# Reading turned tiles back by quarters of the row: one core, two layers of a decoder trunk

## The chip, the core and the metric

The kernel runs on 1 core of one Trainium2 chip. The metric is the device time of one execution in microseconds (us). The profile's engine names are used: PE is TensorE (matmuls; PEld its weight loads), DVE is VectorE, ACT is ScalarE, POOL is GpSimd and SP is SyncE. POOL, SP and ACT also issue transfers (DMAs).

## The reference, cut

Two layers of a decoder trunk with 256 tokens of width 1024, in float32. Each layer: half a SwiGLU block, a token mixer, attention over 256 memory tokens, half a SwiGLU block. Layer 0's mixer joins a gated short convolution with sliding-window attention of 8 heads; layer 1's is causal attention of 8 heads.

```python
def swiglu(x, w_gate, w_up, w_down):
    return (jax.nn.silu(x @ w_gate) * (x @ w_up)) @ w_down
...
for l in range(DEPTH):
    x = x + 0.5 * swiglu(rmsnorm(x, ffn1_norm[l]), ffn1_w_gate[l], ffn1_w_up[l], ffn1_w_down[l])
    h = rmsnorm(x, mix_norm[l])
    if l % 2 == 0:
        i = l // 2
        x = x + even_mixer(h, ev_w_in[i], ev_conv_w[i], ev_sinks[i], ev_w_out[i], rel_bias)
    else:
        i = l // 2
        x = x + odd_mixer(h, od_w_in[i], od_w_out[i], rel_bias)
    x = x + memory_cross_attention(rmsnorm(x, xa_norm[l]), mem_n, xa_w_q[l], xa_w_kv[l], xa_w_o[l])
    x = x + 0.5 * swiglu(rmsnorm(x, ffn2_norm[l]), ffn2_w_gate[l], ffn2_w_up[l], ffn2_w_down[l])
return rmsnorm(x, final_norm)
```

## The kernel before

**Precision by pairs.** Every float32 operand of a matmul is split into two fp32r tiles, hi (a rounded copy, by ACT) and lo (what is left, by DVE), and a product is made of three matmuls: hi by hi, hi by lo, lo by hi. Weights stream from DRAM in 1 MB chunks (`raw`, issued by SP at L117) and are split block by block, 8 tiles of 128x128 at a time, by ACT at L143 (`whi`) and DVE at L144 (`wlo`). Five buffers of each are kept, so ACT and DVE can work up to four blocks ahead of PE, and a split of a block waits until PE has used the block five places before it.

**Feed-forward blocks (`ffn`, four times).** The hidden layer is made with tokens on the partitions, 512 hidden columns at a time (L575 to L577). `turned_back` (L540) then brings it to hidden columns on the partitions, as the down-projection needs. DVE transposes 32x32 blocks inside a tile of 128x1024 (L545); the blocks have still to change places across groups of 32 partitions, so POOL writes the tile to a DRAM buffer `turn` (L547) and reads it back in four transfers that exchange the two block indices (L549). `split` (L553) runs later: ACT (L557) and DVE (L558) make hi and lo tiles `h` of the tile. There are 24 such turns in a run; the last one of each block is 128x512. The last feed-forward block keeps tokens on the partitions for its down-projection too (L792 to L794) and starts it right behind the hidden layer.

**Layer 0's attention (`even_mixer`).** Four head pairs are handled in turn. `attend_two` makes the scores (L1090 to L1092) and the softmax, then `weigh_two` turns the weights in the same way: blocks on DVE (L1033), write of the 128x768 tile `pT` to `pturn` by POOL (L1035), four reads (L1037), then `go_split` on ACT (L1051) and DVE (L1053) into tiles `p`, then `go_weigh`, six matmuls on PE (L1022 to L1024), and the store of the result as an `h` tile (L504, L506). Between these steps PE runs the projections (`group`, L423 to L425: three matmuls of 256 columns for one weight tile), the convolution's and the memory keys' among them. `out_proj` at the end multiplies the eight `h` tiles (four of the convolution, four of the attention) into eight column tiles of the output: first column tiles 0 to 3, then 4 to 7. Four PSUM tiles `acc` are shared by these; `add_to_x` (L486) empties one into the residual `x`.

**What sets the order.** `Order` is a planner: it holds a clock in nanoseconds, a list of filler pieces for PE with estimated costs, and tasks with due times (`pe.after(delay, task, cost)`). When a task is due it goes first, otherwise the next filler. The number 15500 at L1095 is the delay from issuing the reads to `go_split`. The tile framework's scheduler then lays out each engine's instructions, and every engine runs its own in order. POOL's order holds the writes and reads of all turns, with the big accumulated weight transfers of `load_bases` and `add` between them in three of the feed-forward blocks. The splits of a turn are pinned in program order (`tc.keep_in_program_order`). In `out_proj`, `early` cuts the eight inputs: with `()` each column tile takes all eight at once; with `(7,)` column tiles 0 to 3 take the first seven inputs, and then the eighth.

Of the kernel before, what the change touches and what calls it, by code (L numbers as in the profile page):

```python
# [240 lines left out]
def paired(t):  # L241

    return t.rearrange("p (b a) -> p a b", b=2)


def halves(t):

    return t.rearrange("p (b a) -> p b a", b=2)
# [17 lines left out]
def build(nc, tc, ctx, a):  # L266
# [12 lines left out]
    def tr_tile():  # L279
        return psum.tile([P, 512], F32, name="tr", bufs=2)  # L280
# [7 lines left out]
    def p2():  # L288
        return act.tile([P, 512], F32R, name="p2", bufs=4)


    x = consts.tile([P, KT, S], F32, name="x")
# [22 lines left out]
    pe = Order()  # L315
# [173 lines left out]
    def split_into(x2, src):  # L489

        nc.scalar.activation(x2.hi, src, AF.Copy)
        nc.vector.tensor_tensor(x2.lo, src, x2.hi.bitcast(F32), op=ALU.subtract)
        return x2

    def h_tile():
        return Split(act.tile([P, 2 * S], F32R, name="h", bufs=FT))
# [37 lines left out]
    def ffn(which, layer, n, nxt, first=False, last=False):  # L534
# [5 lines left out]
        def turned_back(f0, s, c):  # L540

            t = act.tile([P, 8 * c * 32], F32, name=(("v", "kT", "v", "k2", "kT", "v") if sevens else ("v", "k2") * 3)[f0 // 4], bufs=1)
            to = t.rearrange("p (b u c i) -> p u c b i", b=4, u=2, c=c)
            for u in range(2):
                nc.vector.transpose(to[:, u], s[u].rearrange("p (c b j) -> p c b j", c=c, b=4))  # L545
            d = dram.tile([P, 8 * c * 32], F32, name="turn", bufs=2)
            nc.gpsimd.dma_start(d, t)  # L547
            for b in range(4):
                nc.gpsimd.dma_start(t[32 * b:32 * b + 32].rearrange("j (a x) -> j a x", a=4),  # L549
                                   d.rearrange("(a j) (b x) -> b j a x", a=4, b=4)[b])  # L550
            back = t.rearrange("p (a u c i) -> p c u a i", a=4, u=2, c=c)

            def split():  # L553
                for i in range(c):
                    h[f0 + i] = x2 = h_tile()
                    hi, lo = (m.rearrange("p u (a i) -> p u a i", a=4) for m in (x2.hi, x2.lo))
                    tc.keep_in_program_order(nc.scalar.activation(hi, back[:, i], AF.Copy))  # L557
                    tc.keep_in_program_order(nc.vector.tensor_tensor(lo, back[:, i], hi.bitcast(F32), op=ALU.subtract))  # L558

            pe.after({0: 34000, 4: 34000, 8: 28000, SEVEN: 30000}.get(f0, 26000) if sevens else  # L560
                     28000 if f0 < FT // 4 * 4 - 4 else 22000, split, 0)
# [428 lines left out]
    def weigh_two(prs, v2, store, delay, by_dma):  # L990


        state = {}

        def go_turn():

            if turned:
                pe.after(400, go_turn, 0)
                return
            turned.append(True)  # L1000
            first, last = tr_tile(), tr_tile()
            for s, pr in enumerate(prs):
                for to, at in ((0, 0), (1, 1)):
                    nc.tensor.transpose(first[:, s * S + to * P:s * S + (to + 1) * P], pr[:, at * P:(at + 1) * P], ident)
            for s, pr in enumerate(prs):
                nc.tensor.transpose(last[:, s * P:(s + 1) * P], pr[:, 2 * P:3 * P], ident)
            hi, lo, end = p2(), p2(), p2()
            nc.scalar.activation(hi, first, AF.Copy)
            nc.vector.tensor_tensor(lo, first, hi.bitcast(F32), op=ALU.subtract)
            end = Split(end)  # L1010
            nc.scalar.activation(end.hi, halves(last[:, :S]), AF.Copy)
            nc.vector.tensor_tensor(end.lo, halves(last[:, :S]), end.hi.bitcast(F32), op=ALU.subtract)
            state["pT"] = (paired(hi), paired(lo)), (end.high, end.low)
            pe.after(1600, go_weigh, 1000)

        def go_weigh():
            turned.clear()
            out = tr_tile()
            for t, (ph, pl) in enumerate(state["pT"]):
                ps = out if t == 0 else out[:, S:]  # L1020
                vh, vl = v2(t)
                nc.tensor.matmul(ps, vh, ph, start=t == 0, stop=False)  # L1022
                nc.tensor.matmul(ps, vh, pl, start=False, stop=False)
                nc.tensor.matmul(ps, vl, ph, start=False, stop=t == 1)  # L1024
            store(out.rearrange("p (q s) -> p s q", s=2))
            ws.flush()

        def go_blocks():
            state["t"] = t = act.tile([P, 6 * P], F32, name="pT", bufs=3)
            to = t.rearrange("p (b n i) -> p n b i", b=4, n=6)  # L1030
            for s, pr in enumerate(prs):
                for out, at in ((to[:, 2 * s:2 * s + 2], slice(0, 2 * P)), (to[:, 4 + s:5 + s], slice(2 * P, 3 * P))):
                    tc.keep_in_program_order(nc.vector.transpose(out, pr[:, at].rearrange("p (n b j) -> p n b j", b=4, j=32)))  # L1033
            d = dram.tile([P, 6 * P], F32, name="pturn", bufs=2)
            nc.gpsimd.dma_start(d, t)  # L1035
            for b in range(4):
                nc.gpsimd.dma_start(t[32 * b:32 * b + 32].rearrange("j (a x) -> j a x", a=4),  # L1037
                                   d.rearrange("(a j) (b x) -> b j a x", a=4, b=4)[b])
            pe.after(by_dma, go_split, 0)

        def go_split():
            if turned:
                pe.after(400, go_split, 0)
                return
            turned.append(True)
            back = state["t"].rearrange("p (a n i) -> p n a i", a=4, n=6)
            hi, lo, end = p2(), p2(), Split(p2())
            pairs = [(hi.rearrange("p (n a i) -> p n a i", n=4, a=4), lo.rearrange("p (n a i) -> p n a i", n=4, a=4), back[:, :4]),
                     (*(m.rearrange("p s (a i) -> p s a i", a=4) for m in (end.hi, end.lo)), back[:, 4:])]
            for h, _, src in pairs:  # L1050
                tc.keep_in_program_order(nc.scalar.activation(h, src, AF.Copy))  # L1051
            for h, l, src in pairs:
                tc.keep_in_program_order(nc.vector.tensor_tensor(l, src, h.bitcast(F32), op=ALU.subtract))  # L1053
            state["pT"] = (paired(hi), paired(lo)), (end.high, end.low)
            pe.after(2000, go_weigh, 1000)

        if by_dma:
            pe.after(delay + 200, go_blocks, 0)
        else:
            pe.after(delay, go_turn, 700)  # L1060
# [15 lines left out]
    def attend_two(q, k2, v2, biases, sinks, done):  # L1076

        state = {}

        def go_scores():
            q2 = split_into(q2_tile(), halves(q))
            both = [sc_tile(), sc_tile()]
            for t in range(2):
                ps = both[t][:, :(t + 1) * S]
                kh, kl = (paired(k)[:, :(t + 1) * P] for k in k2)
                qh, ql = (q2.v[:, t, m] for m in range(2))
                nc.tensor.matmul(ps, qh, kh, start=True, stop=False)  # L1090
                nc.tensor.matmul(ps, qh, kl, start=False, stop=False)
                nc.tensor.matmul(ps, ql, kh, start=False, stop=True)  # L1092
            state["p"] = [softmax([ps[:, :(t + 1) * S].rearrange("p (k s) -> p s k", s=2)[:, s] for t, ps in enumerate(both)],
                                  biases[s], sinks[s]) for s in range(2)]
            weigh_two(state["p"], v2, store, 5600, 15500)  # L1095

        def store(out):
            x2 = h_tile()
            parts = [(slice(64 * s, 64 * s + 64), out[64 * s:64 * s + 64, s]) for s in range(2)]
            split_all([(x2.hi[r], x2.lo[r], halves(src)) for r, src in parts])  # L1100
            done(x2)

        pe.after(1400, go_scores, 1000)
# [126 lines left out]
    def even_mixer(n, nxt, bias, sinks, kv2, extra):  # L1230
        k2, v2 = kv2
        o = [None] * 8
# [69 lines left out]
        f = group(W, 0, 2048, n, evac_k) + group(W, 0, 2176, n, evac_v)  # L1302
# [6 lines left out]
            f += t  # L1309
        when_scaled(n, square_scale)  # L1310
        norm_scale(n)
        pe.run(f + extra + out_proj("ev_w_out", 0, o, nxt, ()))

    def odd_mixer(n, nxt, bias, extra):
        k2 = [h_tile() for _ in range(4)]
# [68 lines left out]
    nxt = xn(("mix_norm", 0))  # L1384
# [35 lines left out]
    n, nxt = nxt, xn(("xa_norm", 0))  # L1420
    even_mixer(n, nxt, bias, sinks, kv2_tiles(), mem_keys(0))
    n, nxt = nxt, xn(("ffn2_norm", 0))
    memory(0, n, nxt, keys[0])
    n, nxt = nxt, xn(("ffn1_norm", 1))
    ffn("ffn2", 0, n, nxt)
    n, nxt = nxt, xn(("mix_norm", 1))
    pe.after(114000, lambda: early.update(bias=load_bias(1)), 0)
    ffn("ffn1", 1, n, nxt)
    n, nxt = nxt, xn(("xa_norm", 1))
    odd_mixer(n, nxt, early["bias"], mem_keys(1))  # L1430
    n, nxt = nxt, xn(("ffn2_norm", 1))
# [72 lines left out]
```

## Time and profile before

| what | us |
|---|---|
| median of 3 runs | 954.22 |
| the runs | 954.22, 954.05, 964.56 |
| the profiled execution | 954.28 |
| its span, first to last instruction | 952.5 |
| PE busy in the span | 943.9 |
| DVE busy | 729.8 |
| ACT busy | 597.0 |
| POOL busy | 130.3 |
| mean granted clock of TensorE | 0.998 of full speed |

The page of the profile gives busy time by engine, the span in 40 slices, the transfer queues, the chain of work that ended last, the costliest groups and the transfers by kind. A row of instructions reads: start and duration in us, engine, line, operation, tile written and tiles read, shapes, how many; in brackets the engine's idle time before it and what ended that. A row of a window reads: window, its length, then for PE, PEld, DVE, ACT and POOL the busy us with the count of instructions, then granted clock, share of the transfer engines' time in use, GB/s.

### The profile page before, as it was taken

The numbers are of one execution on the slowest core, as the hardware profiler recorded it, in microseconds if no ns is written. First come the engines' busy times: TensorE is split into PE (matmuls) and PEld (weight loads), VectorE is DVE, ScalarE is ACT, GpSimd is POOL, SyncE is SP. The second block draws the span as 40 slices with busy tenths as digits, with TensorE's granted clock in tenths as the row PEclk, the third lists the DMA queues.
The fourth block names the chain that finished last, engine by engine and source line by source line (L and its number), as shares of the span: only waits on it lengthen the run. The fifth ranks groups of instructions, "written<-read, shape, count | busy, mean of one in ns | idle before, by whom it ended". The sixth has DMA issues, their size and how long they took to land.

```text
span 952.5 us, 15179 instructions
## 1 busy us (share of the span) xinstructions
PE 943.9 (99%) x5772; PEld 865.6 (91%) x5772; DVE 729.8 (77%) x1171; ACT 597.0 (63%) x986; POOL 130.3 (14%) x227
## 2 busy tenths in 40 slices
PE   9999999999999999999999999999999999999997
PEld 8888899999999888889988888999999998888896
DVE  7668667799889886976868697687878798788664
ACT  7545555687568865655577565556786688565551
POOL 0412210022100111121001111200000001112211
PEclk9999999999999999999999999999999999999999
DMA  9999975466547889899768979854644397997861
GB/s 368 322 356 304 336 241 216 164 250 227 167 172 268 239 271 336 258 301 333 238 174 266 333 252 302 282 214 177 228 147 167 121 299 233 287 369 273 265 223 45
DMA packets 40457, 238.60 MB, mean 250 GB/s; under 512 B 5944, under 2 KB 7224, under 8 KB 15808
## 3 DMA queue, kind: packets, MB, share of 16 engines
q1 hardware_dynamic: 26928, 182.43, 53.1%
q0 software_dynamic: 12880, 54.56, 21.6%
q8 instruction: 45, 0.74, 0.3%
q10 hardware_dynamic: 576, 0.64, 0.2%
q14 instruction: 28, 0.23, 0.1%
HBM read 222.38 MB, written 18.37 MB: 253 GB/s over the span
## 4 chain that ended last, share of the span: by engine, by line
PE 93%; DMA 3%; ACT 1%; DVE 1%; issue 0%; POOL 0%; POOLq 0%; DVEq 0%; ACTq 0%
PE acc L576 11%; PE acc L575 11%; PE acc L577 11%; PE acc L418 8%; PE acc L423 7%; PE acc L424 7%; PE acc L425 7%; PE acc L419 4%; PE sc L418 3%; DMA raw<-in_w 2%; PE sc L575 2%; PE sc L576 2%; PE sc L577 2%; PE tr L685 2%; PE tr L686 2%; PE tr L687 2%
## 5 line engine op out<-in xcount | busy, mean ns | idle before, releaser
L144 DVE TENSOR_TENSOR wlo<-raw,whi 128x1024 fp32r<-128x1024 f32 (+2 forms) x365 | 410.8, 1137 | 148.7 <-ACT whi L143 139.7
L143 ACT ACTIVATE whi<-raw 128x1024 fp32r<-128x1024 f32 (+2 forms) x365 | 354.1, 982 | 230.1 <-PE acc L577 88.4
L576 PE MATMUL acc<-wlo,x 128*128 128x512 f32 x528 | 200.8, 380 | 0.3 <-DVE wlo L144 0.3
L577 PE MATMUL acc<-whi,x 128*128 128x512 f32 x528 | 200.1, 380 | 0.0
L575 PE MATMUL acc<-whi,x 128*128 128x512 f32 x528 | 196.6, 381 | 0.0
L576 PEld LDWEIGHTS acc<-wlo,x 128*128 128x128 f32 x528 | 100.0, 189 | 15.4 <-DVE wlo L144 1.4
L577 PEld LDWEIGHTS acc<-whi,x 128*128 128x128 f32 x528 | 100.1, 190 | 14.1
L575 PEld LDWEIGHTS acc<-whi,x 128*128 128x128 f32 x528 | 100.0, 190 | 14.0
L418 PE MATMUL acc<-h,whi 128*128 128x512 f32 x330 | 108.3, 382 | 0.0
L419 PE MATMUL acc<-h,wlo 128*128 128x256 f32 x330 | 89.3, 273 | 0.0
L424 PE MATMUL acc<-h,whi 128*128 128x256 f32 x322 | 87.4, 276 | 0.0
L425 PE MATMUL acc<-h,wlo 128*128 128x256 f32 x322 | 87.2, 275 | 0.0
L423 PE MATMUL acc<-h,whi 128*128 128x256 f32 x322 | 85.8, 277 | 0.0
L424 PE MATMUL acc<-x,whi 128*128 128x256 f32 x304 | 83.9, 277 | 0.0
L425 PE MATMUL acc<-x,wlo 128*128 128x256 f32 x304 | 83.7, 277 | 0.0
L423 PE MATMUL acc<-x,whi 128*128 128x256 f32 x304 | 83.0, 277 | 0.0
L418 PEld LDWEIGHTS acc<-h,whi 128*128 128x128 f32 x330 | 62.1, 189 | 8.4
L419 PEld LDWEIGHTS acc<-h,wlo 128*128 128x128 f32 x330 | 63.3, 192 | 0.4
L424 PEld LDWEIGHTS acc<-h,whi 128*128 128x128 f32 x322 | 61.6, 192 | 0.1
L425 PEld LDWEIGHTS acc<-h,wlo 128*128 128x128 f32 x322 | 61.6, 192 | 0.0
L423 PEld LDWEIGHTS acc<-h,whi 128*128 128x128 f32 x322 | 60.2, 192 | 0.5 <-DVE x L486 0.2
L425 PEld LDWEIGHTS acc<-x,wlo 128*128 128x128 f32 x304 | 58.3, 192 | 0.1
(279 smaller groups left out, 1740.6 us busy)
## 6 DMA issues: line engine op xcount, KB each, us to landing
raw<-in_w SPq DMA_DIRECT2D x165, 1024.0 KB, 6.8
bias<-in_w POOLq DMA_DIRECT2D x12, 1024.0 KB, 12.3
k<-in_w POOLq DMA_DIRECT2D x9, 1024.0 KB, 12.1
turn<-v POOLq DMA_DIRECT2D x9, 512.0 KB, 3.2
v<-turn POOLq DMA_DIRECT2D x36, 128.0 KB, 6.1
dists<-line POOLq DMA_DIRECT2D x2, 1536.0 KB, 13.4
raw<-in_memT SPq DMA_DIRECT2D x3, 1024.0 KB, 4.8
turn<-kT POOLq DMA_DIRECT2D x6, 512.0 KB, 9.3
```

Source lines behind the costliest of these rows:

```text
L143: for ins in (self.nc.scalar.activation(hi[:, at], src, AF.Copy), self.nc.vector.tensor_tensor(lo[:, at], src, hi[:, at].bitcast(F32), op= ...
L144: self.nc.vector.tensor_tensor(lo[:, at], src, hi[:, at].bitcast(F32), op=ALU.subtract)):
L418: nc.tensor.matmul(ps, w[0], x2.both, start=start, stop=False)
L419: nc.tensor.matmul(ps[:, :S], w[1], x2.high, start=False, stop=stop)
L423: nc.tensor.matmul(ps[:, :S], w[0], x2.high, start=start, stop=False)
L424: nc.tensor.matmul(ps[:, :S], w[0], x2.low, start=False, stop=False)
L425: nc.tensor.matmul(ps[:, :S], w[1], x2.high, start=False, stop=stop)
L575: nc.tensor.matmul(ps[u], xh, wh, start=k == 0, stop=False)
L576: nc.tensor.matmul(ps[u], xh, wl, start=False, stop=False)
L577: nc.tensor.matmul(ps[u], xl, wh, start=False, stop=k == KT - 1)
L685: nc.tensor.matmul(ps, xh, wh, start=p == 0, stop=False)
L686: nc.tensor.matmul(ps, xh, wl, start=False, stop=False)
```

## The change

The four reads of a turned tile are cut another way. In both forms a read moves 128 pieces of the DRAM tile, a piece being a quarter of a row. Before, read `b` filled 32 partitions, all four quarters of each (`t[32b:32b+32]`); now read `a` fills one quarter of the row on all 128 partitions. The tile that results is the same. The same edit stands in `turned_back` and in `weigh_two`. Besides, layer 0's `go_split` is due 17500 instead of 15500 ns after the reads are issued, and the out-projection of layer 0 takes column tiles 0 to 3 in two passes, over inputs 0 to 6 and then over input 7.

```diff
@@ turned_back
-            for b in range(4):
-                nc.gpsimd.dma_start(t[32 * b:32 * b + 32].rearrange("j (a x) -> j a x", a=4),
-                                   d.rearrange("(a j) (b x) -> b j a x", a=4, b=4)[b])
+            for a in range(4):
+                nc.gpsimd.dma_start(t.rearrange("p (a x) -> a p x", a=4)[a], d.rearrange("(a j) (b x) -> a b j x", a=4, b=4)[a])
@@ weigh_two, go_blocks: the same edit
...
@@ attend_two
-            weigh_two(state["p"], v2, store, 5600, 15500)
+            weigh_two(state["p"], v2, store, 5600, 17500)
@@ even_mixer
-        pe.run(f + extra + out_proj("ev_w_out", 0, o, nxt, ()))
+        pe.run(f + extra + out_proj("ev_w_out", 0, o, nxt, (7,)))
```

The changed file is two lines shorter, so L1022 before is L1021 after, L1051 is L1049, L549 stays within one line.

On POOL, at the first two head pairs of layer 0 (`pT` is the turned tile, `pturn` its DRAM buffer, `cv` belongs to the convolution), before and then after:

```order
L1035 DMA pturn_2027<-pT_2022 128x768
L1282 TENSOR_TENSOR cv_2166<-w1_2164,cg_2135 128x256
L1037 DMA pT_2022<-pturn_2027 32x4x192 x4
L1035 DMA pturn_2187<-pT_2182 128x768
L1281 MEMSET cv_2586 128x2
L1037 DMA pT_2182<-pturn_2187 32x4x192 x4
```

```order
L1034 DMA pturn_2027<-pT_2022 128x768
L1280 TENSOR_TENSOR cv_2166<-w1_2164,cg_2135 128x256
L1036 DMA pT_2022<-pturn_2027 128x1x192 x4
L1034 DMA pturn_2187<-pT_2182 128x768
L1279 MEMSET cv_2590 128x2
L1036 DMA pT_2182<-pturn_2187 128x1x192 x4
```

Nothing changes place on POOL; only the shape of each read does, 32 partitions by 4 pieces or 128 by one.

On PE, at the first weighing product of the first head pair (`p2` are its split weights, `acc` a projection under way), before and then after:

```order
L423 MATMUL acc_2396<-x_1419,whi_2252 128x256
L424 MATMUL acc_2396<-x_1419,whi_2252 128x256
L425 MATMUL acc_2396<-x_1419,wlo_2253 128x256
L1022 MATMUL tr_2365<-p2_2326,v_1729 128x512
L423 MATMUL acc_2396<-x_1428,whi_2252 128x256
L424 MATMUL acc_2396<-x_1428,whi_2252 128x256
```

```order
L423 MATMUL acc_2365<-x_1428,whi_2252 128x256
L424 MATMUL acc_2365<-x_1428,whi_2252 128x256
L425 MATMUL acc_2365<-x_1428,wlo_2253 128x256
L1021 MATMUL tr_2389<-p2_2341,v_1729 128x512
L423 MATMUL acc_2365<-x_1483,whi_2252 128x256
L424 MATMUL acc_2365<-x_1483,whi_2252 128x256
```

The product stands one weight tile, three matmuls, later.

On DVE, behind the last head pair, where its result (`h`) is stored and the out-projection's first column tiles are added to `x`, before and then after:

```order
L506 TENSOR_TENSOR h_2804<-tr_2797,h_2804 64x2x128 x2
L486 TENSOR_TENSOR x_69<-acc_2817,x_69 128x256
L486 TENSOR_TENSOR x_69<-acc_2852,x_69 128x256
L486 TENSOR_TENSOR x_69<-acc_2887,x_69 128x256
L144 TENSOR_TENSOR wlo_2884<-raw_2731,whi_2883 128x1024
L486 TENSOR_TENSOR x_69<-acc_2922,x_69 128x256
```

```order
L506 TENSOR_TENSOR h_2878<-tr_2871,h_2878 64x2x128 x2
L144 TENSOR_TENSOR wlo_2929<-raw_2795,whi_2928 128x1024
L486 TENSOR_TENSOR x_69<-acc_2794,x_69 128x256
L486 TENSOR_TENSOR x_69<-acc_2818,x_69 128x256
L486 TENSOR_TENSOR x_69<-acc_2847,x_69 128x256
L486 TENSOR_TENSOR x_69<-acc_2899,x_69 128x256
```

A split of a weight block now stands ahead of the first addition, and all four additions follow each other.

More of the change, by code (lines that the diff above doesn't have):

```diff
@@ L1035, in go_blocks @@
             nc.gpsimd.dma_start(d, t)
-            for b in range(4):
-                nc.gpsimd.dma_start(t[32 * b:32 * b + 32].rearrange("j (a x) -> j a x", a=4),
-                                   d.rearrange("(a j) (b x) -> b j a x", a=4, b=4)[b])
+            for a in range(4):
+                nc.gpsimd.dma_start(t.rearrange("p (a x) -> a p x", a=4)[a], d.rearrange("(a j) (b x) -> a b j x", a=4, b=4)[a])
             pe.after(by_dma, go_split, 0)
```

## The prediction

> **What bounds the kernel now.** I read the page's head and its chain of work first, then TensorE's own waits, then a table of windows, then the transfers.
>
> ```profile
> span 952.5 us, 15179 instructions
> PE 943.9 (99%) x5772; PEld 865.6 (91%) x5772; DVE 729.8 (77%) x1171; ACT 597.0 (63%) x986; POOL 130.3 (14%) x227
> PE 93%; DMA 3%; ACT 1%; DVE 1%; issue 0%; POOL 0%; POOLq 0%; DVEq 0%; ACTq 0%
> ...
> PE tr L1022 <- ACT p L1051: 1.0, 1, 1.0
> PE tr L313 <- PEq L1457: 0.8, 1, 0.8
> PE acc L576 <- DVE wlo L144: 0.3, 1, 0.3
> ```
>
> TensorE (PE) is busy 943.9 of 952.5 us, so 8.6 us is everything that a change of waits can ever return. The last three lines (who waited for whom, PE as the waiter: total, times, longest) name only three waits of it: the start, 1.0 us where the attention of layer 0 waits for softmax weights split by ScalarE at L1051, and 0.3 us in a feed-forward block. The windows say the same:
>
> ```profile
> 200.00:225.00 25.00, 23.98 (x204) 23.37 (x204) 21.84 (x61) 20.23 (x56) 7.29 (x14) 1.00 0.58 195
> 300.00:325.00 25.00, 24.93 (x158) 22.86 (x157) 23.50 (x41) 20.74 (x37) 3.94 (x4) 1.00 0.84 265
> 825.00:850.00 25.00, 24.73 (x115) 21.35 (x114) 15.93 (x19) 13.77 (x19) 2.81 (x5) 1.00 1.01 345
> 925.00:950.00 25.00, 21.13 (x145) 19.65 (x143) 14.69 (x25) 7.08 (x15) 6.31 (x5) 0.98 0.09 32
> ```
>
> Second column of figures: PE busy. It lacks 1.02 us at 200 to 225, 0.27 at 825 to 850, and 3.87 in the tail, which the change does not touch. The 1.02 us is at the end of exactly the path that is edited (first head pair; chain of waits in that window):
>
> ```profile
> 205.64 4.14 DMA pturn<-pT
> ...
> 210.07 1.66 POOL pT L1037 x3
> ...
> 211.87 6.86 DMA pT<-pturn
> ...
> 218.83 0.64 ACT p L1051
> ...
> 219.51 0.48 PE tr L1022
> 219.99 0.11 PE acc L423
> 220.10 0.11 PE acc L424
> ```
>
> The turned tile goes to DRAM in 4.14 us, its four reads are issued from 210.07, the last one lands 6.86 us after its issue, ScalarE splits at once, PE follows.
>
> **The reads, part one of the change.** Bytes, number of reads and rows per read stay: four issues, each 128 rows of 768 bytes (L1037) or 1024 and 512 (L549). POOL's order is the same row for row, so nothing passes anything there or on SP. What changes is which 128 rows belong to one read: 32 partitions by 4 pieces before, 128 partitions by one piece now. Every user of the tile reads all of it and so waits for all four reads in both forms. The whole question is by how much the last of the four lands later or earlier; I call that d. Rows that bound it (issue to landing: quartet min/median/max, and medians over the run):
>
> ```profile
> DMA to landing us min/median/max: 3.6/6.1/6.9
> ...
> DMA to landing us min/median/max: 2.4/2.7/3.0
> ...
> raw<-in_w SPq DMA_DIRECT2D x165, 1024.0 KB, 6.8
> turn<-v POOLq DMA_DIRECT2D x9, 512.0 KB, 3.2
> v<-turn POOLq DMA_DIRECT2D x36, 128.0 KB, 6.1
> ```
>
> The first line is the first head pair's quartet (210 to 212.4 us), the second that of the second pair (219.7 to 222), when few other transfers run. So d cannot be better than 3.0 - 6.9 = -3.9 us. The upper end is the rival below, +2.4. Between them: a 512 KB write from all 128 partitions lands in 3.2 us, a 128 KB read into 32 partitions in 6.1 (other windows, other direction), which leans to spreading being no worse. I take a small gain, d = -0.35 us, and keep both ends.
>
> [...]
>
> **Where d reaches PE.** (a) First head pair. In the new order PE's first weighing product stands three matmuls later, at 0.11 us each: 0.33 us of the 1.02 is covered whatever d is. ScalarE's row of L1051 stands where it stood, since it was waiting for the landing anyhow. Left is 0.69 + d. With d = -0.35: 0.34. Term: -0.33 - 0.35 = -0.68 us; ends -1.02 and, at d = +2.4, +2.07.
>
> (b) The feed-forward turns. ScalarE waits there too, longest near the end:
>
> ```profile
> 899.90 1.34 ACT L557 ACTIVATE h<-kT 128x256 fp32r<-128x256 f32 x4 [7.57 <-DMA kT<-turn]
> 901.14 3.88 ACT L143 ACTIVATE whi<-raw 128x1024 fp32r<-128x1024 f32 x4
> ...
> 906.36 2.00 ACT L143 ACTIVATE whi<-raw 128x1024 fp32r<-128x1024 f32 x2
> 909.41 1.06 ACT L143 ACTIVATE whi<-raw 128x1024 fp32r<-128x1024 f32 x1 [1.06 <-PE acc L794]
> ...
> 902.22 4.63 DVE L144 TENSOR_TENSOR wlo<-raw,whi 128x1024 fp32r<-128x1024 f32 x4 [0.43 <-ACT whi L143]
> ...
> 904.25 0.38 PE L793 MATMUL acc<-wlo,h 128*128 128x512 f32 x1
> ```
>
> The four weight blocks queued behind that 7.57 us wait are what PE eats next. The first wlo of the four ends at 902.22 + 4.63/4 = 903.4; PE needs it at 904.25. (That it is this one: 909.41 waits for the buffer of five blocks before, two blocks at 906.36 lie between, so the first of the four at 901.14 is PE's block before the one just freed, begun 904.03.) So PE has 0.85 us to spare: an earlier landing gains nothing here, a later one costs d - 0.85. Term at my d: 0. The other long wait is in the first feed-forward block:
>
> ```profile
> 79.73 1.34 ACT L557 ACTIVATE h<-k 128x256 fp32r<-128x256 f32 x4 [4.36 <-DMA k<-turn]
> 81.28 1.05 ACT L143 ACTIVATE whi<-raw 128x1024 fp32r<-128x1024 f32 x1
> ...
> 82.36 1.23 DVE L144 TENSOR_TENSOR wlo<-raw,whi 128x1024 fp32r<-128x1024 f32 x1 [0.41 <-ACT whi L143]
> ...
> 86.94 1.06 ACT L143 ACTIVATE whi<-raw 128x1024 fp32r<-128x1024 f32 x1 [0.62 <-PE acc L577]
> ```
>
> The block split at 81.28 has its wlo at 83.59 and, being four before that of 86.94, is begun by PE near 86.9: 3.3 us to spare. Term 0.
>
> (c) The 0.27 us at 825 to 850 is a weight load that came late in a window where transfers are saturated (share 1.01 in its row). The reads move the same bytes there. Term 0, ends -0.27 and a few tenths.
>
> **Later split and out-projection, part two.** The planner's due time of the split grows by 2 us (15500 to 17500). For pairs 1 and 2 the row on ScalarE does not move. For pair 3 it moves behind one weight split and one key split, and PE's weighing with it, about 18 matmuls, some 2 us. Pair 4 is weighed later by 25 matmuls, and the out-projection no longer needs it first: with (7,) its first four column tiles run over seven inputs, then over the eighth. Pairs 2 to 4 made no wait before and have more cover now: 0. What is new is at the seam:
>
> ```profile
> 253.54 0.28 PE L1024 MATMUL tr<-p,v 128*128 128x256 f32 x1
> ...
> 253.86 0.77 ACT L504 ACTIVATE h<-tr 64x256 fp32r<-64x256 f32 x2 [2.26 <-PE tr L1024]
> ...
> 257.88 1.09 DVE L486 TENSOR_TENSOR x<-acc,x 128x256 f32<-128x256 f32 x3 [2.36 <-PE acc L425]
> ```
>
> Four column tiles now end within 12 matmuls, and the fifth needs the first one's accumulator, freed by L486. Counted from pair 4's last product: PE wants it 34 matmuls on, 3.74 us. VectorE gets there over the ScalarE stores (0.32 + 0.77), a weight split on ScalarE (1.06) and its rest on VectorE (1.23), which now stands ahead of L486, and 1.09/3 for L486: 3.74. Within a few hundredths, so term +0.1, ends 0 and +0.5. The same seam in the memory layer (one last input, four tiles) costs at most the 0.07 us that 300 to 325 lacks.
>
> **Sum.** The profiled execution took 954.28 us (span 952.5 and 1.8 around it), the median of the three is 954.22. 954.28 - 0.68 + 0 + 0 + 0.1 = 953.7.
>
> **Rivals.** *One read runs on a quarter of the transfer engines.* The new source is written as 4 groups of 32 rows; if a transfer is dealt out by its outermost count, each read sits on 4 engines, the four reads side by side, and an engine carries 32 KB of one read instead of 8 KB. By the 512 KB write, 32 KB an engine in 3.2 us, 24 KB more cost at most 2.4 us; by the raw loads, 64 KB in 6.8, 2.6. At least 1.0 us, by the fastest slice of the page:
>
> ```profile
> GB/s 368 322 356 304 336 241 216 164 250 227 167 172 268 239 271 336 258 301 333 238 174 266 333 252 302 282 214 177 228 147 167 121 299 233 287 369 273 265 223 45
> ```
>
> (373 / 16 = 23 GB/s an engine). Then (a) gives +0.67 to +2.07, (b) +0.15 to +1.55: 955.1 to 957.9, say 956.0. For it: the written shape, which alone earns it about a quarter. Against it: every read of before has 32 or more as its outermost count, so no row shows that transfers are dealt out by it. [...]
>
> *Slower by over 2%: all four reads on the same four engines.* Then 128 KB an engine instead of 32: d from 4.2 us (96 KB at 23 GB/s) to 9.6 (at 32 KB per 3.2 us). At 9.6, (a) +9.3, (b) +8.8 and +6.3, and pairs 3 and 4 some 7 each: 954.3 + 38 = 992. It decides once d exceeds about 6. Against it: that would leave 12 engines idle in the middle of a turn.
>
> *The change does nothing:* ScalarE's waits shift, d is near 0, and only the three matmuls count: 954.0.
>
> *A new wait takes the old one's place:* the accumulator seam at its upper end, with d = 0: 954.28 - 0.33 + 0.5 = 954.5.
>
> **Chances.** Forecast (953.3 to 953.9) 0.50; does nothing 0.13; new wait 0.09; four engines 0.24; over 2% slower 0.04. The range runs from both waits gone (954.28 - 1.02 - 0.27 = 953.0, less a tenth) to 957.0, leaving out the last, the upper third of four engines and a little below. The likeliest one's own range is 952.9 to 954.2. Two per cent, 19 us, is about what a measurement of this kernel tells from no change; faster by that is excluded by the 8.6 us of idle PE, so 0.01, slower 0.04, within 0.95.
>
> **What would show it.** Right: the wait of PE at L1021 (L1022 before) is 0 to 0.5 us, the four reads of the first pair land 6 to 7 us after issue, ScalarE's wait near 900 us is 7.5 or less. Wrong: landings longer by 1 us or more and PE rows that wait for whi or wlo near 904 us (four engines), or for L486 near 257 us (the seam). Wrong too if PE's busy sum leaves 943.9 by over 1 us, since no matmul is added or removed.

## The result, and the profile after

| | before | after |
|---|---|---|
| median, us (13 runs each) | 954.22 | 964.11 |
| lowest and highest | 953.3 to 964.56 | 960.19 to 968.61 |
| span of the profiled execution | 952.5 | 962.3 |

After / before is 1.0102, 95% interval 1.0085 to 1.0119: slower by one per cent, 7 us above the upper end of the forecast's range. The profiled execution of after took 964.11 us.

The page's head of after, with the counts of engines' work and of transfers:

```profile
span 962.3 us, 15180 instructions
PE 946.8 (98%) x5772; PEld 866.3 (90%) x5772; DVE 730.6 (76%) x1171; ACT 597.5 (62%) x986; POOL 144.9 (15%) x227
...
DMA packets 49929, 238.77 MB, mean 248 GB/s; under 512 B 15544, under 2 KB 16632, under 8 KB 25280
```

The same line on transfers in the page of before:

```profile
DMA packets 40457, 238.60 MB, mean 251 GB/s; under 512 B 5944, under 2 KB 7224, under 8 KB 15808
```

Two things leap out. The data are nearly the same (238.77 against 238.60 MB), but there are 9472 packets more, all of the growth below 512 bytes. And PE's span grew by 9.8 us, of which 2.9 is busy time and 6.9 is waiting (15.5 us idle against 8.6). Who waited for whom on PE in after (total, times, longest):

```profile
PE acc L791 <- ACT whi L143: 2.8, 1, 2.8
PE tr L1021 <- ACT p L1049: 1.8, 1, 1.8
PE acc L575 <- DVE wlo L144: 1.6, 2, 0.8
PE acc L574 <- ACT whi L143: 1.3, 2, 0.8
...
PE acc L792 <- DVE wlo L144: 0.8, 1, 0.8
```

The windows of after put these waits in three places (columns as in the table of before):

```profile
200.00:225.00 25.00, 23.19 (x195) 22.44 (x194) 20.85 (x59) 19.11 (x52) 8.73 (x14) 1.00 0.59 190
825.00:850.00 25.00, 22.20 (x100) 18.33 (x99) 12.63 (x16) 10.05 (x16) 3.39 (x5) 1.00 1.02 328
900.00:925.00 25.00, 21.42 (x91) 17.91 (x90) 11.64 (x14) 10.46 (x15) 6.33 (x10) 0.93 0.74 210
```

In before the third place had:

```profile
900.00:925.00 25.00, 25.00 (x135) 22.40 (x134) 16.42 (x19) 15.50 (x26) 4.77 (x8) 1.00 0.68 231
```

PE's idle time goes from 1.02 to 1.81 us at the first head pair, from 0.27 to 2.80 at 825 to 850, and from 0 to 3.58 at 900 to 925: 0.79 + 2.53 + 3.58 = 6.9. The third place has a granted clock of 0.93 as well, against 1.00 before.

The reads themselves, issue to landing in after: the quartet of the first head pair, then that of the second.

```profile
DMA to landing us min/median/max: 7.5/7.8/8.0
...
DMA to landing us min/median/max: 3.9/4.1/4.1
```

And the medians over the run, for writes and for reads of a feed-forward turn:

```profile
turn<-v POOLq DMA_DIRECT2D x9, 512.0 KB, 3.3
v<-turn POOLq DMA_DIRECT2D x36, 128.0 KB, 8.3
```

Against medians of 6.1, 2.7 and 6.1 us before. The second pair's quartet runs nearly alone (from 219.7 to 226 us the share of the transfer engines' time in use is 0.32 in before and 0.40 in after), so its 1.4 us is the price of the new form there; the written tile (`turn<-v`), untouched by the change, is as fast as before (3.3 us against 3.2).

What the extra packets are is seen by sorting the records of POOL's queue by size:

```text
bytes a packet:   4096  4608  1536     4   16   24   32    8
before            6400   256   256  2744    0    0    0    8
after             6400   320    64  2744 7680  960  768  200
```

A 128 KB read of a feed-forward turn has 32 data packets of 4096 bytes (four rows) in both forms. In after, 96 packets of 16 bytes come with them (7680 over 80 reads): three small ones for each data packet, 4 bytes for each row in it. A read of a head pair was 16 packets of 4608 and 16 of 1536 bytes, which is 16 shares of 8 rows; now it is 20 and 4, which is 4 shares of 32 rows, again with three small packets for each. So a read's data are in 4 shares, and 12 shares are filled with packets of almost nothing. The landings say the same. The trace keeps sixteen landing marks for each transfer (5792 for 362 issues, in before and in after): for the first read of the second pair they stand 2.06 to 3.02 us behind its issue in before, while in after twelve stand at 1.81 to 1.97 and four at 3.58 to 3.94. The shares of the four reads are not on one and the same set of four: of the data packets of the second pair's reads up to 13 are in flight at the same time (17 in before).

### The profile page after: what moved, and what is told of

The parts are those of the page before. It is cut to its first block, busy times and chain, and to the rows that moved or that the text cites. A ratio compares the mean times of both kernels' runs of the same rounds, so it can differ in the third digit from the quotient of the medians.

```text
span 962.3 us, 15180 instructions
## 1 busy us (share of the span) xinstructions
PE 946.8 (98%) x5772; PEld 866.3 (90%) x5772; DVE 730.6 (76%) x1171; ACT 597.5 (62%) x986; POOL 144.9 (15%) x227
## 2 busy tenths in 40 slices
DMA packets 49929, 238.77 MB, mean 248 GB/s; under 512 B 15544, under 2 KB 16632, under 8 KB 25280
## 4 chain that ended last, share of the span: by engine, by line
PE 90%; DMA 5%; ACT 2%; DVE 1%; issue 1%; POOL 0%; POOLq 0%; DVEq 0%; ACTq 0%
PE acc L575 11%; PE acc L574 11%; PE acc L576 11%; PE acc L418 7%; PE acc L423 7%; PE acc L424 7%; PE acc L425 6%; PE acc L419 4%; PE sc L418 3%; DMA raw<-in_w 2%; PE sc L574 2%; PE sc L575 2%; PE sc L576 2%; PE tr L684 2%; PE tr L686 2%; PE tr L685 2%
```

## Experiments

Each changes the kernel before in one way, the last in two. Ratios are to the kernel before on the same chip.

**1. The reads alone, and the order alone.** The diff is each half of the change by itself.

> The new reads in both places, with the split due after 15500 ns and the out-projection in one pass, as before. Theory 'reads' (the reads' new form makes the last of four land later and gives all of the 9.9 us): 962 to 966 us, with 9472 more packets than before and PE stalls of 2 to 4 us near 843 and 910 us. Theory 'order' (the later split and the two passes of the out-projection cost the time): 953 to 955, no such stalls. If both share it: in between.

> The reads of before, with the split due after 17500 ns and the out-projection's tiles 0 to 3 in two passes. Theory 'reads': 953.5 to 954.5 us, PE waits 0 to 0.7 us for the first pair's weights (0.33 of the 1.02 covered), 40457 packets as before. Theory 'order': 960 to 964.

Measured: reads alone 964.77 us, ratio 1.0106 (1.0066 to 1.0146), with 49929 packets. Order alone 953.80, ratio 0.9993 (0.9970 to 1.0015). PE's waits with the order alone:

```profile
PE tr L1022 <- ACT p L1051: 0.6, 1, 0.6
PE tr L1023 <- DVE p L1053: 0.3, 1, 0.3
```

The wait of 1.02 us became 0.63, but with 0.26 for the lo part behind it 0.89 in all. The seam lies in the window of 250 to 275 us, here in before and then with the order alone:

```profile
250.00:275.00 25.00, 25.00 (x222) 24.79 (x221) 19.78 (x35) 14.61 (x25) 0.00 (x0) 1.00 0.53 188
```

```profile
250.00:275.00 25.00, 24.87 (x220) 24.60 (x220) 19.96 (x37) 15.33 (x27) 0.00 (x0) 1.00 0.56 206
```

PE lacks 0.13 us there that it did not lack before, at the fifth column tile (0.14 in after). The whole loss belongs to the reads.

**2. Is it 128 partitions, or the 4 groups?** Three forms of the four reads that part the two (the added lines alone). All three leave out the exchange of the blocks; bytes, number of reads and their order stay:

```diff
@@ plain128: 128 partitions, source of 128 rows
+            for a in range(4):
+                nc.gpsimd.dma_start(t.rearrange("p (a x) -> a p x", a=4)[a], d.rearrange("p (a x) -> a p x", a=4)[a])
@@ four32: 32 partitions, source of 4 groups of 8 rows (eight32: r=5, [:, :4], dv[8 * b:8 * b + 8])
+            dv = d.rearrange("(g r) w -> g r w", r=9)[:, :8]
+            nc.gpsimd.dma_start(dv, t)
+            for b in range(4):
+                nc.gpsimd.dma_start(t[32 * b:32 * b + 32], dv[4 * b:4 * b + 4])
```

> Each of the four reads fills one quarter of the row on all 128 partitions, as after, but from the same quarter of the same 128 rows of the DRAM tile, so that the source is 128 rows instead of 4 groups of 32. It leaves out the exchange of the blocks; the rest is before. Theory 'engines' (4 as the outermost count puts a read on 4 of 16 engines): 128 rows go to 16 engines, so no small packets beside the data, reads of the second pair land in about 2.5 to 3 us after issue as before, 953 to 955 us. Theory 'shape' (one row on 128 partitions is dearer than four on 32): landings and time as after, 961 to 966.

> Each of the four reads fills 32 partitions with whole rows of the DRAM tile (4 KB pieces, so a quarter as many), and the DRAM tile has a gap behind every 8 rows, so that the source of a read is 4 groups of 8 rows. It leaves out the exchange of the blocks; the rest is before. Theory 'engines': 4 groups put each read on 4 engines although it fills 32 partitions; three small packets for every data packet, landings longer than before by 1 us or more, 959 to 966 us. Theory 'shape': 32 partitions are filled as before, 953 to 955 us, no small packets.

> As the run with 4 groups of 8 rows, but with a gap behind every 4 rows, so that the source of a read is 8 groups of 4 rows; the exchange of the blocks is left out. Theory 'engines by the outermost count': a read sits on 8 engines, one small packet for every data packet, landings between those of before and of 4 groups, 954 to 959 us. Theory 'gaps' (any source in pieces with gaps is put on 4 engines or is slow): as with 4 groups, 962 to 968.

| form | source's outermost count | partitions of a read | us | ratio and interval | small packets for a data packet | second pair's quartet, median us |
|---|---|---|---|---|---|---|
| before | 32 | 32 | 954.2 | | 0 | 2.7 |
| plain128 | 128 | 128 | 953.69 | 0.9997 (0.9980 to 1.0014) | 0 | 2.5 |
| eight32 | 8 | 32 | 953.44 | 0.9991 (0.9982 to 1.0001) | 1 | 2.7 |
| four32 | 4 | 32 | 965.92 | 1.0127 (1.0068 to 1.0186) | 3 | 3.4 |
| after | 4 | 128 | 964.11 | 1.0102 (1.0085 to 1.0119) | 3 | 4.1 |

The transfers of plain128, of eight32 and of four32, in this order:

```profile
DMA packets 40457, 238.60 MB, mean 251 GB/s; under 512 B 5944, under 2 KB 7224, under 8 KB 15808
...
v<-turn POOLq DMA_DIRECT2D x36, 128.0 KB, 5.0
```

```profile
DMA packets 43273, 238.61 MB, mean 251 GB/s; under 512 B 9016, under 2 KB 10040, under 8 KB 18624
...
v<-turn POOLq DMA_DIRECT2D x36, 128.0 KB, 6.1
```

```profile
DMA packets 49417, 238.64 MB, mean 247 GB/s; under 512 B 15160, under 2 KB 16184, under 8 KB 24768
...
v<-turn POOLq DMA_DIRECT2D x36, 128.0 KB, 10.1
```

The small packets and the time follow the groups, not the partitions: with 8 groups each data packet has one small companion, with 4 groups three, which is what 8 and 4 shares out of 16 would give. The sixteen landing marks of the second pair's first read agree: eight at 1.49 to 1.82 us and eight at 2.30 to 3.02 with 8 groups, twelve at 1.51 to 1.67 and four at 3.15 to 3.34 with 4. Filling 128 partitions costs nothing by itself: two kinds of read land sooner than before (`v<-turn` 5.0 us against 6.1, `kT<-turn` 6.5 against 7.6), two as before (`k<-turn` 6.3 against 6.2, `pT<-pturn` 4.4 and 4.4). Data in 8 of the 16 shares cost nothing that can be measured here (953.44 us, ratio 0.9991; the expectation for eight32 had allowed up to 959), data in 4 of them cost one per cent (ratios 1.0102 and 1.0127). What POOL pays to issue is not the main cause: an issue took 0.67 us in after and 0.57 in four32, against 0.55 before, and four32 is as slow as after.

**3. Which turns cost the time?** The new reads in some places only (a condition on `last`, on `f0`, or on the function):

> The new reads in the last feed-forward block alone (6 of 24 turns); the rest is before, the attention too. Theory 'last block' (only there does a late turn reach PE: a stall near 843 us by a late weight load and one near 910 us by a late turn): 960 to 964 us. Theory 'every turn' (each of the 28 turns gives its share): 956 to 957.

> The new reads in the first three feed-forward blocks (18 of 24 turns), the reads of before in the last block and in the attention. Theory 'last block': 954 to 955.5 us, though these turns' reads land later by 1 to 5 us, since their splits are due later still. Theory 'every turn': 959 to 961.

> The new reads in the last three turns of the last feed-forward block alone. Theory 'chain' (on POOL's queue the reads of turn 4, the write of turn 5 and the reads of turn 5 follow one another, and each lands later, so that ScalarE's wait near 900 grows by 3 to 5 us and PE stalls there): a stall of 2 to 4 us near 905 to 910 and slower matmuls behind it, none near 843; 957 to 960 us. Theory 'first stall' (the second stall comes of the first, which makes everything late): 954 to 955.5.

> The new reads in the first three turns of the last feed-forward block alone. Theory 'late weights' (the 2.5 us that PE lost at 825 to 850 us come of these turns' reads, which hold a few engines longer while weight loads share them): stalls of 1 to 3 us between 835 and 850, none near 910; 955.5 to 958.5 us. Rival (the loss there is chance, or comes from the blocks ahead): 954 to 955, at most the 0.3 us of before lost there.

> The new reads in the attention of layer 0 alone (4 of 28 turns), all else as before. Theory 'engines': the first pair's last read lands 0 to 1 us later, so PE's wait there grows from 1.02 to 1.2 to 2.0 us, and nothing else changes: 954.4 to 955.5 us. Rival: the attention's turns carry more than their number, 956 or more.

| new reads in | us | ratio and interval |
|---|---|---|
| last feed-forward block (6 turns) | 962.91 | 1.0084 (1.0067 to 1.0101) |
| its first three turns | 957.67 | 1.0036 (1.0013 to 1.0058) |
| its last three turns | 957.90 | 1.0038 (1.0018 to 1.0058) |
| the first three blocks (18 turns) | 958.55 | 1.0041 (1.0021 to 1.0061) |
| the four head pairs | 957.29 | 1.0025 (1.0008 to 1.0043) |

For the first of these there is no profile to read.

Most of the loss is made in the last block, but "only there" is wrong: the eighteen turns of the first three blocks were expected to cost at most 1.2 us and cost 0.41%, 3.9 us; the head pairs at most 1.0, and they cost 2.4. The parts sum to 0.25 + 0.41 + 0.84 = 1.5%, all reads together cost 1.06%: what is lost early seems to give later turns time. That last clause is argued, not tested.

The last block's two losses are separate. With its first three turns alone, the window of 825 to 850 us:

```profile
825.00:850.00 25.00, 23.16 (x99) 19.43 (x98) 14.11 (x18) 11.71 (x16) 4.13 (x6) 0.93 1.02 340
900.00:925.00 25.00, 25.00 (x128) 22.16 (x127) 14.85 (x17) 13.04 (x17) 4.76 (x8) 1.00 0.88 282
```

PE loses 1.84 us there and nothing at 900. With the last three turns alone, ScalarE's waits for turned tiles and PE's waits:

```profile
896.55 1.34 ACT L561 ACTIVATE h<-k 128x256 fp32r<-128x256 f32 x4 [7.65 <-DMA k<-turn]
908.74 1.33 ACT L561 ACTIVATE h<-kT 128x256 fp32r<-128x256 f32 x4 [8.96 <-DMA kT<-turn]
```

```profile
PE acc L796 <- ACT whi L143: 5.7, 1, 5.7
PE acc L797 <- DVE wlo L144: 1.2, 2, 0.8
```

There is no wait near 843, and 5.7 us near 911, more than the 2 to 4 expected. This execution was the slowest of its ten (965.2 of 954.98 to 965.2). The fourth read of turn 4 took 15.9 us to land in it, fifteen of its sixteen marks being there after 9.0, and 8.1 in after: how late the last share comes varies, and so does the time.

The profile of new reads in the first three blocks (the slowest of its six executions, 962.06 us) has a stall in the first block too, in the window of 75 to 100 us:

```profile
75.00:100.00 25.00, 22.94 (x108) 19.59 (x106) 16.41 (x21) 11.67 (x17) 6.64 (x10) 1.00 0.78 231
```

PE lacks 2.06 us there, in the block for which the prediction counted 3.3 us to spare. In the profile of after that stall did not come. In the same profile PE lacks 1.63 us at 900 to 925 as well, at a clock of 0.93, although the last block has the reads of before there. So it is not shown that what this execution lost was lost at the eighteen turns alone. The head pairs alone, at their place:

```profile
200.00:225.00 25.00, 23.16 (x187) 22.79 (x186) 20.93 (x59) 19.39 (x53) 8.28 (x14) 0.93 0.59 188
```

The wait grew from 1.02 to 1.84 us, inside the expected 1.2 to 2.0. What the expectation left out is the clock of 0.93 behind it, 25 x 0.07 = 1.75 us of slower products, and 0.40 us that PE lacks at the fourth pair (24.60 of 25 us busy at 250 to 275).

**4. The exchange made by the writes.** The tile goes out in four writes of 32 partitions that place the quarters, and comes back in one read of 512 KB into 128 partitions. The result is the same as before. `turned_back` is shown; `weigh_two` has the same edit.

```diff
-            nc.gpsimd.dma_start(d, t)
-            for b in range(4):
-                nc.gpsimd.dma_start(t[32 * b:32 * b + 32].rearrange("j (a x) -> j a x", a=4),
-                                   d.rearrange("(a j) (b x) -> b j a x", a=4, b=4)[b])
+            for a in range(4):
+                nc.gpsimd.dma_start(d.rearrange("(a b j) x -> a j b x", a=4, b=4)[a],
+                                   t[32 * a:32 * a + 32].rearrange("j (b x) -> j b x", b=4))
+            nc.gpsimd.dma_start(t.rearrange("p (a x) -> p a x", a=4), d.rearrange("(a p) x -> p a x", a=4))
```

> The exchange is made by the writes: four writes from 32 partitions each, which place the quarters, then one read of 512 KB that fills all 128 partitions from 4 runs of 128 rows (the DRAM tile is laid out by quarters). Every transfer has 32 or 128 as its outermost count, so by theory 'engines' all sit on 16 engines and no small packets appear: 953 to 955 us. Rival: four writes in a row and one long read make the turn longer than one write and four short reads, stalls near 900 us as after: 957 or more.

> The same with the split due after 17500 ns and the out-projection in two passes. If the one long read lands sooner than the last of four, the first pair's wait of 1.02 us at PE is gone or below 0.4 us: 952.8 to 954.2 us, a little below before. Rival as in the run without the later split: 957 or more.

Measured: 952.58 us, ratio 0.9975 (0.9960 to 0.9989), and with the later order 952.16, ratio 0.9970 (0.9959 to 0.9982). Both beat before and after. Head, two transfers and the one wait of PE that the list of the second names:

```profile
span 950.0 us, 15134 instructions
PE 942.9 (99%) x5772; PEld 865.8 (91%) x5772; DVE 730.5 (77%) x1171; ACT 597.2 (63%) x986; POOL 135.7 (14%) x227
...
turn<-v POOLq DMA_DIRECT2D x36, 128.0 KB, 4.9
v<-turn POOLq DMA_DIRECT2D x9, 512.0 KB, 7.4
```

```profile
PE tr L313 <- PEq L1457: 0.8, 1, 0.8
```

Beyond the start PE lacks only the 0.14 us of the seam here (24.86 of 25 us at 250 to 275). ScalarE's split of the first pair began at 216.57 us, against 218.83 in before. With the two waits gone in both versions, the later order adds nothing that can be told apart (the intervals overlap).

## Why the prediction was wrong, point by point

**The step that failed is d**, the shift of the last landing, "a small gain, d = -0.35 us". At the first pair d was +1.1 us, in the quiet place of the second pair the median landing rose by 1.4. The lean to spreading did no harm: reads of 128 partitions without small packets land no later (plain128: 5.0 against 6.1 us, 2.5 against 2.7 in the quiet place). Its support was thin, though: the 3.2 us of `turn<-v` is the fastest of three rows of 512 KB writes in before, `turn<-kT` having 9.3 and `turn<-k` 10.1. But the form of the source, which the prediction held to be a rival with 0.24, decides (ratio 0.9997 in plain128, 1.0127 in four32). With outermost counts of 4, 8, 32 and 128 at the source the runs had 3, 1, 0 and 0 small packets for a data packet. The prediction said that no row of before shows that transfers are dealt out by that count, since every read there had 32 or more. One small transfer of before does: `line<-kT`, 24 KB with 8 rows outermost on both sides, stands in the trace as 8 packets of 3072 bytes with 8 of 8 bytes beside them, the same 4 bytes for each piece. The sign was there to be read, and 0.24 was too low.

**The rival's own price was too small as well**: 955.1 to 957.9 us against 964.1. Its terms:

*(a) First head pair*, +0.67 to +2.07: measured +0.79 of PE's idle time. Right: 1.80 - 0.69 makes d 1.1 us there, within the +1.0 to +2.4 of that rival. Of this, 0.24 us is POOL's longer issue (its fourth read goes out 2.04 us behind the first, 1.80 before). That three matmuls cover 0.33 us holds for the first product where the order alone was changed (1.02 to 0.63), but the wait of 0.26 for the lo part took most of it back, and the sum had no term for that.

*(b) Last block, "costs d - 0.85"*, +0.15 to +1.55: measured 3.58. The slack was right, but d was counted for one turn, and three transfers stand in a row on POOL. POOL's rows of turns 4 and 5 in before:

```profile
871.01 0.56 POOL L547 DMA_DIRECT2D turn<-k  x1 [3.54 <-DVE k L545]
879.50 2.19 POOL L549 DMA_DIRECT2D k<-turn  x4 [7.94 <-ACT whi L143]
882.27 0.56 POOL L547 DMA_DIRECT2D turn<-kT  x1 [0.58 <-DVE kT L545]
891.17 0.56 POOL L549 DMA_DIRECT2D kT<-turn  x1 [8.34 <-ACT h L557]
```

and in after, with ScalarE's row that waits for the last of them:

```profile
875.03 0.59 POOL L547 DMA_DIRECT2D turn<-k  x1 [2.86 <-DVE k L545]
884.96 2.64 POOL L549 DMA_DIRECT2D k<-turn  x4 [9.34 <-issue]
887.59 0.59 POOL L547 DMA_DIRECT2D turn<-kT  x1
897.83 2.64 POOL L549 DMA_DIRECT2D kT<-turn  x4 [9.65 <-ACT whi L143]
```

```profile
908.68 1.33 ACT L556 ACTIVATE h<-kT 128x256 fp32r<-128x256 f32 x4 [10.26 <-DMA kT<-turn]
```

From the write of turn 4 to its reads 8.49 us became 9.93 (+1.44), from these to the write of turn 5 2.77 became 2.63 (-0.14), from that write to its reads 8.90 became 10.24 (+1.34), and from the reads to ScalarE's split 8.73 (899.90 - 891.17) became 10.85 (+2.12): +4.76 in all. The write of 512 KB, unchanged in itself, is late too: in the same queue it landed 2.08 us behind the last read of turn 4 (1.80 before). PE, which wanted its block at 904.25 before, got it at 912.27, 8.02 later. Its last product ahead of the stall began at 907.83, against 903.82 before, so it came there 4.01 late already, and the split, 8.78 late, was 4.77 late against it. 4.77 - 0.85 = 3.9. PE lost 8.02 - 4.01 = 4.0 there: 3.58 of idle time, and 0.4 that counts as busy.

*(c) The late weight load*, "term 0, ends -0.27 and a few tenths": measured +2.53. "The reads move the same bytes there" was true and not enough. The chain of waits shows the load, in before and then in after:

```profile
820.65 18.89 DMA raw<-in_w
```

```profile
821.33 22.22 DMA raw<-in_w
...
843.63 1.07 ACT whi L143
```

It took 22.2 us to land, 3.3 longer than before, in a stretch where the transfer engines are fully in use (share 1.02, and 1.01 before). That the reads of the first three turns alone make this stall is what first_turns shows; how they do it is open. One candidate is that the load ends with the slowest of the engines: its sixteen landing marks stand 17.6 to 18.9 us behind the issue in before and 16.3 to 22.2 in after. But in first_turns they stand at 19.5 to 20.7, so there the load is late as a whole. The other candidate is POOL's own 1 MB loads, which stand behind the first turn's reads: `bias<-in_w` is issued at 824.06 in before, at 829.54 in after and at 825.92 in first_turns, and in all three the weight load lands 0.2 to 0.3 us behind it; in first_three, though, it lands 6.1 us ahead of it.

*A term that was missing*: PE's clock. The prediction held PE's busy sum fixed at 943.9; it rose by 2.9. The chain of after behind the stall of 3.58 us:

```profile
912.27 0.48 PE acc L792
912.75 0.22 PE acc L793
...
913.46 0.43 PE acc L793
...
916.02 0.43 PE acc L793
...
916.82 0.22 PE acc L792
```

For some 3 us the same products take 0.43 us, not 0.22. Two short windows give the clock of this stretch (third figure from the end):

```profile
910.00:915.00 5.00, 3.21 (x10) 2.44 (x11) 4.57 (x6) 3.80 (x5) 4.91 (x8) 0.82 0.43 118
915.00:920.00 5.00, 5.00 (x21) 4.26 (x20) 3.75 (x5) 3.40 (x5) 0.00 (x0) 0.84 0.98 290
```

At 0.82 and 0.84 the products lose 5 x 0.18 + 5 x 0.16 = 1.7 us, which is 3.4 us at half the clock (from 913.3 to 916.6 us the granted clock is 0.50). The other 1.2 us of busy time goes with the waits: the product ahead of one is counted with 0.38 us where the next otherwise begins 0.22 after it, and the one behind it has 0.32 to the next begin (912.27 to 912.59), some 0.26 us a wait. After has five such waits more than before at these two places, so about 1.3 us (an estimate from these rows). The three idle times and this add up to the loss: 0.79 + 2.53 + 3.58 + 2.9 = 9.8. The clock was halved behind waits of 2.80 and 0.78 us with one product between them. The length of the waits alone does not settle it: 1.84 us of waiting went with a clock of 0.93 in two windows of experiment 3 (825 to 850 of first_turns, 200 to 225 of pair_reads), while 1.81 us at 200 to 225 of after, and 2.80 in pieces at 825 to 850, left it at 1.00. What decides is open.

**Part two** was right but for the lo part: 0 for pairs 2 to 4, and 0.13 to 0.14 us at the seam (term +0.1). The profile puts that wait of after down to L486, as predicted.

**What would show it.** The signs that had been named for "wrong" came: landings longer by 1 us and more, PE waiting for whi and wlo behind 904 us, a busy sum more than 1 us off. The wait at L1021, expected at 0 to 0.5, was 1.8.

**The other rivals.** "All four reads on the same four engines" did not come: 13 data packets at once. "Does nothing" and "accumulator seam" would have been 954.0 and 954.5; the order alone gave 953.8, which its interval (0.9970 to 1.0015) does not tell from either.

## What to carry to other kernels

Look at the outermost count of a transfer's pattern. In these runs a count of 4 at the source put a read's data into 4 of 16 shares and cost one per cent (ratios 1.0102 and 1.0127), though bytes and number of reads stayed; a count of 8 put them into 8 and cost nothing (0.9991). The small packets in the profile's count gave it away (9472 packets more in after). The forms here with 32 or more outermost on both sides had none for their data; moving the exchange from the reads into the writes kept to that and gave the version that beats both (952.58 us). When a transfer gets slower, count it as often as it stands in a row on its queue (three in a row made ScalarE's split 4.77 us late against PE in the last block), look at what else is under way on the transfer engines (the weight load there took 22.2 us, 18.9 before), and add slower matmuls behind a stall (0.43 us instead of 0.22 for some 3 us).

## What the runs showed that was not expected

- A read with its data in 4 of 16 shares came with packets of 4 bytes for each row in the 12 others: 9472 more packets in after, 0.17 MB.
- Data in 8 of 16 shares were as good as in all 16 here: 953.44 us, ratio 0.9991.
- Moving the exchange into the writes gained 2.4 us by its ratio against before, though only 1.3 of PE's waits (1.02 and 0.27) were there to be won; PE's busy sum is 1.2 lower too (942.7 against 943.9). Which part of that version gives what was not tried.
- A stall went with nearly as much loss again by the clock: in four32 PE lacks 5.77 us at 900 to 925 (19.23 of 25 busy), and at the granted clock of 0.80 there the products lose another 25 x 0.20 = 5.0 us (an estimate from that window).
